# Both feed-forward down projections as seven 2x2 block products over pairs of hidden tiles, with norms by quarters of the tokens

## The chip, the cores and the metric

The kernel runs on one core of a Trainium2 chip, in one launch. The metric is the device time of one execution in microseconds, the median of several runs. TensorE (PE) multiplies, VectorE (DVE), ScalarE (ACT) and GpSimd (POOL) do elementwise work, SyncE (SP) issues nearly all DMAs.

## The reference

One decoder layer over 1024 prompt tokens and 8 single-token samples (1032 columns in all), model width 1024, in float32: a half feed-forward, a token mixer (RWKV-7 and RG-LRU), cross-attention, a second half feed-forward, each followed by a layer norm. The change concerns the two feed-forwards and the norms behind them:

```python
D_MODEL = 1024; D_FF = 2816; DN_ALPHA = 2.0 ** 0.25
def _swiglu(h, wi, wo):
    u = h @ wi
    gate, up = u[..., :D_FF], u[..., D_FF:]
    return (jax.nn.silu(gate) * up) @ wo
h = _layer_norm(DN_ALPHA * h + 0.5 * _swiglu(h, ffn1_wi, ffn1_wo), ln_g[0], ln_b[0])
...
h = _layer_norm(DN_ALPHA * h + 0.5 * _swiglu(h, ffn2_wi, ffn2_wo), ln_g[3], ln_b[3])
```

## The kernel before

Activations lie transposed, features on the 128 partitions and tokens along the free axis: `S.acc` (float32) and its split `S.HH`, `S.HL` are each 8 tiles of 128 x 1032. Every operand of a product is split into a high and a low part in the fp32r type: ACT copies the high part, DVE subtracts it from the raw value (`split`, L225 to L229; `split_half`, L90 to L100), and `mm3` (L122 to L127) issues three matmuls per product, high x high, high x low, low x high. A raw tile comes by DMA into one of a few `raw` buffers.

`ffn` works in two stages. The up projection takes hidden tiles in pairs (`pair`): the 2x2 blocks of weights and activations are combined so that seven block products (the "forms" B11, B21, T1, B22, T2, T3, T4) do the work of eight. POOL forms the weight sums of a pair (`pool_tt`, L334), a product has 258 columns (`HN`, a quarter of the tokens), DVE adds the forms up and multiplies gate by up, and SP writes each finished hidden tile to `HID` in DRAM (L407). A first pair (`classic`) is done without forms, woven with the preceding norm.

The down projection goes tile by tile. The 22 hidden tiles are cut into 8 groups of 2 or 3 (`groups`). `loads` fetches and splits the next group's hidden rows (into HH and HL, for the last group into tiles of its own, `hh` and `hl`) and its weights, while the products of the present one run. For each of 8 output tiles and 3 token thirds of 344 columns (`CH3`) a group is summed in PSUM; the first group is copied, scaled, into `acc` by ACT (L440), the others are added by DVE (L442). Between groups 2 and 5, POOL adds the residual `src`, reloaded by SP, to `acc` (L464). Last, `down_last` takes the last group third by third, and each third's norm is woven with the products of the next one (`weave` steps its streams in proportion).

A norm (`ln_stream`): the sum over feature tiles (L145) goes through a matmul with `ones_d` (L169); DVE subtracts the mean (L181), ACT squares, POOL or DVE adds pairs of squares (L185), PE sums them (L176), a few small steps give the inverse deviation (L192 to L195), PE transposes it (L200), DVE scales (L205), ACT adds the bias (L207); then either the result is written out (second feed-forward) or ACT and POOL split it into HH and HL (L214, L215), which the mixer's products read.

The order within an engine is the order of its queue. It comes from a scheduler that runs over the program in its written order; pools with few buffers (`raw`, `whl`, `xw`, PSUM banks) decide how far loads run ahead. There is no planner of due times.

Of the kernel before, what the change touches and what calls it, by code (L numbers as in the profile page):

```python
# [10 lines left out]
F32 = mybir.dt.float32  # L11
# [8 lines left out]
NT = NP + NS  # L20
# [115 lines left out]
def ln_stat_step(S, st, m, c0, n):  # L136
# [4 lines left out]
    if m == 1:  # L141
        st.s = S.lnp.tile([128, n], F32, tag="lns", name="lns")
# [17 lines left out]
def ln_stream(S, st, li, c0, n, final, keep):  # L160
# [11 lines left out]
    adds = nc.gpsimd if final is None or c0 + n < NT else nc.vector  # L172
# [6 lines left out]
    for k in range(KT):  # L179
        d = acc[:, k, c0:c0 + n]  # L180
        nc.vector.tensor_tensor(out=d, in0=d, in1=mu[:, :n], op=ALU.subtract)  # L181
        sq.append(S.lnp.tile([128, 344], F32, tag="lnq", name="lnq", bufs=3))
# [100 lines left out]
def ffn(S, octx, wi, wo, li, src, pre=(), final=None, keep=None, after=None):  # L283
# [5 lines left out]

    nc, tc = S.nc, S.tc  # L290
    HID = S.dram.tile([JT, 128, NT], F32, name="HID%d" % li)
    with ExitStack() as ctx:
# [39 lines left out]
        gt = pool(uctx, "fg", 6)  # L332
        TT = lambda o, a, b, op: nc.vector.tensor_tensor(out=o, in0=a, in1=b, op=op)
# [30 lines left out]
        def pair(j):  # L364
# [46 lines left out]
        groups = [[0, 1]] + [[3 * g + i for i in (2, 3, 4)] for g in range(5)] + [[17, 18], [19, 20, 21]]  # L411
        hd, wt = {}, {}
        S.hlseq = itertools.cycle([S.whl] * 2 + [S.hlx] * 2)

        def loads(js, to=None):
            for j in js:
                hd[j] = to() if to else (S.HH[:, j % KT, :], S.HL[:, j % KT, :])
                for p in range(2):
                    N = slice(2 * HN * p, 2 * HN * p + 2 * HN)
                    x = raw_tile(S)  # L420
                    nc.sync.dma_start(out=x, in_=HID[j, :, N])
                    split(nc, [t[:, N] for t in hd[j]], x)
                wt[j] = load_split(S, wo[128 * j:128 * j + 128, :])

        loads(groups[0])
        uctx.close()
        S.norms = Norms(S, octx)
        hlast = pool(ctx, "fhl", 3)
        xw = pool(ctx, "fwo", 5)
        S.hlseq = itertools.cycle([S.hlx] * 2 + [xw] * 2 + [S.whl] * 3 + [xw] * 3 + [S.hlx] * 2)  # L430

        def down_tile(js, m, ni, st=None):
            c0, n = CH3[ni]
            q = psum(n)
            for j in js:
                hh, hl = hd[j]
                mm3(nc, q, wblock(wt[j], m), hh[:, c0:c0 + n], hl[:, c0:c0 + n], j == js[0], j == js[-1])
# [5 lines left out]
            if st is not None:  # L443
                ln_stat_step(S, st, m, c0, n)
# [1286 lines left out]
```

## Time and profile before

| | us |
|---|---|
| median of 3 runs (lowest, highest) | 3210.02 (3202.42, 3212.22) |
| the profiled execution, own time | 3199.62 |
| its span | 3197.8 |
| PE busy | 3017.8 (94%) |
| DVE busy | 2197.6 (69%) |
| ACT busy | 1432.7 (45%) |
| POOL busy | 560.2 (18%) |

The profiled execution lies 10.4 us under the median of the runs. A row of the timeline gives an instruction's start and duration in us, counted from the start of the span; a name such as `ps<-HH,wh` is the output and the inputs by the program's names. PE overlaps successive matmuls, so their pitch is read from starts, or from the count in a stretch in which PE is busy all the time. The granted clock (PEclk) is a share of the full 2.4 GHz.

### The profile page before, as it was taken

How to read it: one execution, taken by the hardware profiler on the slowest of the kernel's cores; microseconds unless marked ns; L12 is line 12 of the kernel's file. 1: busy time of each engine (PE TensorE's matmuls, PEld its weight loads, DVE VectorE, ACT ScalarE, POOL GpSimd, SP SyncE). 2: the span in 40 equal slices, each digit the busy share in tenths (PEclk: the TensorE clock that was granted, in tenths of full speed). 3: DMA queues.
4: the chain of work that ended last, by engine and by line, in shares of the span. 5: the costliest groups of instructions: out<-in, count | busy, mean ns of one | idle time of the engine just before them, and what ended most of it. 6: DMA issues, size and time to landing. Idle time of an engine off the chain costs nothing. (4 is left out here: it accounts for less than half of the span.)

```text
span 3197.8 us, 63225 instructions
## 1 busy us (share of the span) xinstructions
PE 3017.8 (94%) x23324; PEld 2848.3 (89%) x23324; DVE 2197.6 (69%) x5895; ACT 1432.7 (45%) x3195; POOL 560.2 (18%) x526
## 2 busy tenths in 40 slices
PE   8999999999999999999999979889997999999997
PEld 8999999999888898888878768778887999999997
DVE  7666665574366888877777877666767666666556
ACT  5333342125465565566555645364235433334212
POOL 2222200132010111010001000250005322220111
PEclk9999999999999999999998969799999999999998
DMA  4222243314644554545454445554433222225321
GB/s 138 80 80 77 80 162 107 110 50 136 207 128 131 152 143 137 143 129 150 138 143 126 131 139 149 178 175 136 150 120 116 71 80 80 80 80 159 107 86 54
DMA packets 391301, 386.72 MB, mean 121 GB/s; under 512 B 153904, under 2 KB 292176, under 8 KB 390992
## 3 DMA queue, kind: packets, MB, share of 16 engines
q1 hardware_dynamic: 390992, 382.69, 39.7%
q8 instruction: 183, 3.00, 0.4%
q14 instruction: 126, 1.03, 0.1%
HBM read 277.54 MB, written 105.23 MB: 120 GB/s over the span
## 5 line engine op out<-in xcount | busy, mean ns | idle before, releaser
L125 PE MATMUL ps<-HH,wh 128*128 128x258 f32 (+1 forms) x2384 | 718.8, 302 | 16.9 <-ACT HH L510 7.4
L126 PE MATMUL ps<-HL,wh 128*128 128x258 f32 (+1 forms) x2384 | 716.9, 301 | 0.1
L127 PE MATMUL ps<-HH,wl 128*128 128x258 f32 (+1 forms) x2384 | 715.8, 300 | 0.0
L125 PE MATMUL g<-HH,wh 128*128 128x344 f32 (+2 forms) x1840 | 624.3, 340 | 14.2 <-DVE acc L442 3.4
L127 PE MATMUL g<-HH,wl 128*128 128x344 f32 (+2 forms) x1840 | 596.2, 325 | 0.5 <-DVE wl L100 0.5
L126 PE MATMUL g<-HL,wh 128*128 128x344 f32 (+2 forms) x1840 | 594.5, 324 | 0.6 <-POOL HL L215 0.5
L125 PEld LDWEIGHTS ps<-HH,wh 128*128 128x128 f32 x2384 | 451.6, 190 | 19.2 <-ACT HH L510 7.4
L126 PEld LDWEIGHTS ps<-HL,wh 128*128 128x128 f32 x2384 | 451.2, 189 | 0.6 <-DVE HL L511 0.5
L127 PEld LDWEIGHTS ps<-HH,wl 128*128 128x128 f32 x2384 | 450.4, 189 | 0.0
L125 PEld LDWEIGHTS g<-HH,wh 128*128 128x128 f32 x1840 | 357.5, 194 | 33.5 <-ACT wh L99 4.6
L126 PEld LDWEIGHTS g<-HL,wh 128*128 128x128 f32 x1840 | 357.8, 195 | 5.3 <-POOL HL L215 1.4
L127 PEld LDWEIGHTS g<-HH,wl 128*128 128x128 f32 x1840 | 355.7, 194 | 4.6 <-DVE wl L100 0.9
L228 ACT ACTIVATE wh<-raw 128x512 fp32r<-128x512 f32 x280 | 176.5, 631 | 321.7 <-PE ps L126 262.5
L334 POOL TENSOR_TENSOR raw<-raw 128x512 f32<-128x512 f32 x160 | 214.1, 1338 | 566.4 <-DVE wl L229 360.1
L229 DVE TENSOR_TENSOR wl<-raw,wh 128x512 fp32r<-128x512 f32 x280 | 201.7, 721 | 137.9 <-ACT wh L228 131.0
L100 DVE TENSOR_TENSOR wl<-raw,wh 128x512 fp32r<-128x512 f32 x302 | 218.7, 731 | 99.9 <-ACT wh L99 97.8
L99 ACT ACTIVATE wh<-raw 128x512 fp32r<-128x512 f32 x302 | 184.6, 625 | 220.1 <-PE ps L126 110.5
L442 DVE SCALAR_TENSOR_TENSOR acc<-ps,acc 128x344 f32<-128x344 f32 x336 | 168.6, 512 | 142.3 <-PE ps L127 141.3
L550 DVE TENSOR_TENSOR pr<-tq,iv 128x2 f32<-128x2 f32 (+30 forms) x496 | 159.8, 322 | 3.2
L555 ACT ACTIVATE ev<-g 128x344 f32<-128x344 f32 x192 | 86.9, 453 | 135.8 <-PE g L127 126.9
L948 DVE TENSOR_REDUCE tq<-pr 128x1 f32<-128x2 f32 (+30 forms) x496 | 120.9, 244 | 2.9
L555 ACT ACT_TABLE_LOAD x93 | 119.3, 1283 | 6.9 <-DVE cs L550 2.9
(410 smaller groups left out, 6303.2 us busy)
## 6 DMA issues: line engine op xcount, KB each, us to landing
raw<-in_wi_dram SPq DMA_DIRECT2D x176, 256.0 KB, 2.6
raw<-in_w_in_dram SPq DMA_DIRECT2D x116, 256.0 KB, 3.3
GD<-ev SPq DMA_DIRECT2D x168, 172.0 KB, 2.5
raw<-in_wo_dram SPq DMA_DIRECT2D x104, 256.0 KB, 3.6
raw<-HID SPq DMA_DIRECT2D x88, 258.0 KB, 3.9
HID<-g SPq DMA_DIRECT2D x80, 258.0 KB, 2.1
tg<-GD SPq DMA_DIRECT2D x32, 512.0 KB, 3.8
wt<-T SPq DMA_DIRECT2D x160, 64.0 KB, 2.8
```

The lines of the kernel that those rows point to most:

```text
L99: nc.scalar.activation(out=hi, in_=raw, func=AF.Identity)
L100: S.low.tensor_tensor(out=lo, in0=raw, in1=hi.bitcast(F32), op=ALU.subtract)
L125: nc.tensor.matmul(ps, wh, xh, start=first, stop=False)
L126: nc.tensor.matmul(ps, wh, xl, start=False, stop=False)
L127: nc.tensor.matmul(ps, wl, xh, start=False, stop=last)
L228: nc.scalar.activation(out=hi, in_=x, func=AF.Identity)
L229: nc.vector.tensor_tensor(out=lo, in0=x, in1=hi.bitcast(F32), op=ALU.subtract)
L334: pool_tt = lambda o, a, b, op: nc.gpsimd.tensor_tensor(out=o, in0=a, in1=b, op=op)
L442: nc.vector.scalar_tensor_tensor(out=a, in0=q, scalar=0.5 / ALPHA, in1=a, op0=ALU.mult, op1=ALU.add)
L550: TTo = lambda o, a, b, op: nc.vector.tensor_tensor(out=o, in0=a, in1=b, op=op)
L555: ACT = lambda o, a, f=AF.Identity, **kw: nc.scalar.activation(out=o, in_=a, func=f, **kw)
L948: nc.vector.tensor_reduce(out=tq[:, 0:m, i], in_=pv, axis=mybir.AxisListType.X, op=ALU.add)
```

## The change

The down projection takes the hidden tiles as 11 pairs and the same seven forms. Of a pair the 2x2 hidden blocks (tile of the pair x left or right quarter of a token half) and the 2x2 weight blocks (tile of the pair x left or right half of the output) are combined. The hidden combinations are formed where the hidden tiles are made (`hidden`, POOL), and all seven go to DRAM as `HF`. Form by form, over two sets of pairs (6, then 5), `prepare` loads and splits the hidden blocks and the weights; the weight sums of T1 are formed by POOL in a buffer `room.w` ("fw") that T2 to T4 read, that of B22 by POOL from a fresh load. A form's products of a set are summed in PSUM, per output tile m (4), token half p (2), and `add` brings the result to `acc`, which now starts as a copy of the residual `src` loaded by 8 DMAs. `room.u` holds the partial sum that several output blocks share. The last two forms of the second set go quarter by quarter with the norms (`finish`), now four norms of 258 columns; `ahead`, which loads the next stage's first weight, comes before the last of them.

```diff
-            for m in range(2):
-                for p in range(2):
-                    nc.sync.dma_start(out=HID[j + m, :, 2 * HN * p:2 * HN * p + 2 * HN], in_=G[m][p])
+            hidden(j // 2, G)
+        def hidden(i, G):
+            T = [ft.tile([128, 2 * HN], F32, tag="t%d" % t, name="t%d" % t) for t in range(4)]
+            sub = lambda o, a, b: pool_tt(o, a, b, ALU.subtract)
+            for p in range(2):
+                (b11, b12), (b21, b22) = ((g[p][:, :HN], g[p][:, HN:]) for g in G)
...
+                for f, b in ((0, b11), (1, b21), (3, b22)):
+                    nc.sync.dma_start(out=HF[i, f, :, N], in_=b)
+                sub(t1, b12, b11)
+                sub(t3, b22, b12)
+                sub(t2, b22, t1)
+                sub(t4, t2, b21)
+            for f, t in zip((2, 4, 5, 6), T):
+                nc.sync.dma_start(out=HF[i, f], in_=t)
...
+        FORMS = ("B11", "B21", "T1", "B22", "T2", "T3", "T4")
+        groups = [range(6), range(6, JT // 2)]
...
+        def prepare(g, f):
+            for n, i in enumerate(groups[g]):
+                x = raw_tile(S)
+                nc.sync.dma_start(out=x, in_=HF[i, f])
...
+                split(nc, hid, x)
+                x = lambda: raw_tile(S)[:, :512]
+                if f < 2:
+                    w = fetch(x(), i, 11 + 10 * f)
+                elif form == "T1":
+                    a11, a21, a22 = (fetch(room.w[:, 3 * n + t], i, b) for t, b in enumerate((11, 12, 22)))
+                    w = x()
+                    pool_tt(w, a21, a22, ALU.add)
+                    pool_tt(a21, a11, a21, ALU.subtract)
+                    pool_tt(a11, a22, a21, ALU.subtract)
+                elif form == "B22":
+                    w = fetch(x(), i, 21)
+                    pool_tt(w, w, room.w[:, 3 * n], ALU.subtract)
+                else:
+                    w = room.w[:, 3 * n + FORMS.index(form) - 4]
+                res.append((wparts(w), hid))
...
+        def add(f, q, m, p, last):
...
+            scaled = lambda o: nc.scalar.activation(out=o, in_=q, func=AF.Identity, scale=sc)
+            onto = lambda o, s=sc: nc.vector.scalar_tensor_tensor(out=o, in0=q, scalar=s, in1=o, op0=ALU.mult,
+                                                                 op1=ALU.add)
+            also = lambda o, x, by=pool_tt: by(o, o, x, ALU.add)
+            if form == "B11":
+                scaled(u)
+                also(c11, u)
+            elif form == "B21":
+                onto(c11)
+            elif form == "T1":
+                v = room.v.tile([128, HN], F32, tag="v", name="v")
+                scaled(v)
+                also(c12, v)
+                also(c22, v)
+            elif form == "B22":
+                onto(c12)
+            elif form == "T2":
+                onto(u)
+                also(c12, u)
+            elif form == "T3":
+                onto(u)
+                also(c22, u, TT if last else pool_tt)
+                also(c21, u)
+            else:
+                onto(c21, -sc)
...
+        for k in range(KT):
+            nc.sync.dma_start(out=S.acc[:, k, :], in_=src[k])
...
+            for p, m in itertools.product(range(2), range(4)):
+                add(f, product(ops, m, p), m, p, False)
...
-        for ni in range(3):
+        for p, f in itertools.product(range(2), (5, 6)):
+            if p and f == 6 and after is not None:
+                ahead(S, after)
             st = SimpleNamespace()
-            weave((down_last(groups[-1], ni, st), KT), *pre)
-            pre = [(ln_finish(S, st, li, *CH3[ni], final, keep), LN_STEPS)]
+            weave((finish(f, p, st), 4), *pre)
+            pre = [(ln_finish(S, st, li, 2 * HN * p + HN * (6 - f), HN, final, keep), LN_STEPS)]
```

POOL's queue before, from the end of the first up projection through its down projection to the first norm of the thirds (`raw` at L334: weight sums of the up projection; L464: the residual; L145 and L185: the norm):

```order
L334 TENSOR_TENSOR raw<-raw 128x512 x77
L464 TENSOR_TENSOR acc<-acc,raw 128x516 x16
L622 MEMSET TT_8799 128x512
L622 MEMSET TT_8800 128x512
L145 TENSOR_TENSOR lns<-lns,acc 128x344
```

Here the only work in the down projection is the sixteen additions of the residual. POOL's queue in the changed kernel, from the last hidden combination (`t3`) to the first weights of T1 (`pool_tt` stands at L337 there; `fu` is `room.u`, `fw` is `room.w`, and the `raw` tile written from `fw` is T1's own weight):

```order
L337 TENSOR_TENSOR t3_6215<-t1_6213,g_5685 128x258
L337 TENSOR_TENSOR acc_6304<-acc_6304,fu_6318 128x258 x8
L337 TENSOR_TENSOR raw_6568<-fw_6314 128x512
L337 TENSOR_TENSOR fw_6314<-fw_6314 128x512 x2
L337 TENSOR_TENSOR raw_6583<-fw_6314 128x512
L337 TENSOR_TENSOR fw_6314<-fw_6314 128x512 x2
L337 TENSOR_TENSOR raw_6598<-fw_6314 128x512
```

The eight additions of B11's result stand ahead of T1's weights, and each of T1's six weight sums is followed by the two sums for T2 and T3. The same queue a little later, from T1's last weight on (`v` is T1's result, added to two output blocks; the `raw` tiles written from `raw` and `fw` are B22's weights):

```order
L337 TENSOR_TENSOR raw_6643<-fw_6314 128x512
L337 TENSOR_TENSOR fw_6314<-fw_6314 128x512 x2
L337 TENSOR_TENSOR acc_6304<-acc_6304,v_6896 128x258 x2
L337 TENSOR_TENSOR acc_6304<-acc_6304,v_6919 128x258 x2
L337 TENSOR_TENSOR raw_6815<-raw_6815,fw_6314 128x512
L337 TENSOR_TENSOR acc_6304<-acc_6304,v_6942 128x258 x2
L337 TENSOR_TENSOR acc_6304<-acc_6304,v_6965 128x258 x2
L337 TENSOR_TENSOR raw_6826<-raw_6826,fw_6314 128x512
L337 TENSOR_TENSOR raw_6837<-raw_6837,fw_6314 128x512
L337 TENSOR_TENSOR acc_6304<-acc_6304,v_6988 128x258 x2
```

B22's weights stand between the additions of T1's results. SP's queue before, at the change from the first up projection to its down projection (L407 writes a hidden tile, L421 loads one back, L94 loads half a weight tile):

```order
L407 DMA HID0_131<-g_5488 128x516
L421 DMA raw_6338<-HID0_131 128x516
L407 DMA HID0_131<-g_5489 128x516
L94 DMA raw_6342<-in_wo1_dram 128x512
L94 DMA raw_6348<-in_wo1_dram 128x512
L421 DMA raw_6354<-HID0_131 128x516
```

SP's queue in the changed kernel at the same place (L419 and L425 write hidden forms, L461 loads one, L447 loads a weight block, L538 the residual):

```order
L419 DMA HF0_132<-g_5685 128x258
L425 DMA HF0_132<-t3_6215 128x516
L461 DMA raw_6373<-HF0_132 128x516
L447 DMA raw_6377<-in_wo1_dram 128x512
L461 DMA raw_6383<-HF0_132 128x516
L538 DMA acc_6304<-in_xT_dram 128x1032 x8
L447 DMA raw_6387<-in_wo1_dram 128x512
L461 DMA raw_6561<-HF0_132 128x516
L447 DMA fw_6314<-in_wo1_dram 128x512 x3
L461 DMA raw_6576<-HF0_132 128x516
L447 DMA fw_6314<-in_wo1_dram 128x512 x6
```

The eight loads of `acc` stand behind the last write of a hidden form and ahead of the first load of `fw`.

## Rows read from the trace of the kernel before

**Rows 1.** The page's head and its busy times by engine (us, share, instructions).
```profile
span 3197.8 us, 63225 instructions
...
PE 3017.8 (94%) x23324; PEld 2848.3 (89%) x23324; DVE 2197.6 (69%) x5895; ACT 1432.7 (45%) x3195; POOL 560.2 (18%) x526
```

**Rows 2.** Windows: busy us and count by engine, clock, DMA share, GB/s.
```profile
core 0: us, PE busy (x) PEld busy (x) DVE busy (x) ACT busy (x) POOL busy (x), PEclk, DMA share, GB/s
160.00:240.00 80.00, 80.00 (x669) 80.00 (x668) 52.78 (x100) 29.05 (x59) 20.99 (x16) 1.00 0.25 80
480.00:640.00 160.00, 160.00 (x1016) 160.00 (x1016) 90.51 (x163) 34.11 (x61) 16.43 (x12) 1.00 0.35 108
```

**Rows 3.** Timeline of PE: start, us, instruction, count, idle before and its releaser.
```profile
460.07 0.32 PE L125 MATMUL ps<-HH,wh 128*128 128x344 f32 x1
...
467.92 0.42 PE L125 MATMUL ps<-HH,wh 128*128 128x344 f32 x1 [2.02 <-ACT acc L440]
...
678.10 0.32 PE L125 MATMUL ps<-hh,wh 128*128 128x344 f32 x1
...
723.76 0.40 PE L127 MATMUL ps<-hh,wl 128*128 128x344 f32 x1
727.59 0.66 PE L125 MATMUL g<-HH,wh 128*128 128x344 f32 x1 [3.43 <-DVE acc L442]
...
3128.29 0.32 PE L125 MATMUL ps<-hh,wh 128*128 128x344 f32 x1
```

**Rows 4.** Timeline of POOL in the first and the second up projection.
```profile
424.27 1.28 POOL L334 TENSOR_TENSOR raw<-raw 128x512 f32<-128x512 f32 x1 [5.64 <-DVE wl L229]
...
2480.66 0.74 POOL L246 TENSOR_TENSOR acc<-acc 128x258 f32<-128x258 f32 x1
```

**Rows 5.** The page's costliest groups: count, busy us, mean ns, idle before.
```profile
L228 ACT ACTIVATE wh<-raw 128x512 fp32r<-128x512 f32 x280 | 176.5, 631 | 321.7 <-PE ps L126 262.5
L334 POOL TENSOR_TENSOR raw<-raw 128x512 f32<-128x512 f32 x160 | 214.1, 1338 | 566.4 <-DVE wl L229 360.1
L229 DVE TENSOR_TENSOR wl<-raw,wh 128x512 fp32r<-128x512 f32 x280 | 201.7, 721 | 137.9 <-ACT wh L228 131.0
```

**Rows 6.** Timeline of DVE at the end of the first up projection.
```profile
462.83 0.42 DVE L333 TENSOR_TENSOR g<-g,c 128x258 f32<-128x258 f32 x1
```

**Rows 7.** The page's DMA issues: count, KB each, median us to landing.
```profile
HID<-g SPq DMA_DIRECT2D x80, 258.0 KB, 2.1
```

**Rows 8.** Windows of 10 us with the most DMA traffic; columns as before.
```profile
10.00:20.00 10.00, 8.74 (x47) 7.90 (x47) 7.26 (x16) 8.31 (x17) 0.00 (x0) 1.00 1.04 342
460.00:470.00 10.00, 7.98 (x51) 7.70 (x51) 7.05 (x15) 6.17 (x14) 0.00 (x0) 1.00 0.88 289
```

**Rows 9.** Timeline of POOL and DVE where the residual is added.
```profile
572.04 1.68 POOL L464 TENSOR_TENSOR acc<-acc,raw 128x516 f32<-128x516 f32 x1 [1.05 <-DVE acc L442]
572.49 1.78 DVE L100 TENSOR_TENSOR wl<-raw,wh 128x512 fp32r<-128x512 f32 x1
```

**Rows 10.** Windows behind the end of the first down projection; columns as before.
```profile
725.00:730.00 5.00, 2.41 (x7) 2.22 (x8) 3.95 (x11) 5.00 (x13) 3.75 (x4) 0.63 0.72 251
730.00:735.00 5.00, 5.00 (x23) 4.71 (x22) 4.13 (x6) 5.00 (x12) 4.47 (x6) 0.69 0.47 147
```

**Rows 11.** Timeline of DVE and ACT in the last norm of the kernel.
```profile
3178.83 1.78 DVE L181 TENSOR_TENSOR acc<-acc,ln 128x344 f32<-128x344 f32 x4 [0.40 <-PE ln L169]
...
3184.92 0.52 DVE L185 TENSOR_TENSOR lnq<-lnq 128x344 f32<-128x344 f32 x1 [0.76 <-ACT lnq L183]
...
3189.71 2.02 DVE L205 SCALAR_TENSOR_TENSOR acc<-acc,lng,ln 128x344 f32<-128x344 f32 x4 [2.48 <-PE ln L200]
...
3194.32 0.58 ACT L207 ACTIVATE acc<-acc,lnb 128x344 f32<-128x344 f32 x1 [0.21 <-DVE acc L205]
```

**Rows 12.** Lines of DVE by form: count, busy us, mean ns, idle before.
```profile
L205 DVE SCALAR_TENSOR_TENSOR acc<-acc,lng,ln 128x344 f32<-128x344 f32 x48 | 24.9, 566 | 10.5 <-PE ln L200 10.5
L205 DVE SCALAR_TENSOR_TENSOR acc<-acc,lng,ln 128x256 f32<-128x256 f32 x48 | 20.7, 470 | 4.0 <-PE ln L200 4.0
```

**Rows 13.** Timeline of PE and POOL in the first feed-forward's last norm.
```profile
710.34 0.82 PE L169 MATMUL ln<-lns,ones_d 128*128 128x344 f32 x2
...
726.25 7.87 POOL L215 TENSOR_TENSOR HL<-acc,HH 128x344 fp32r<-128x344 f32 x8 [3.40 <-ACT HH L214]
```

More of the change, by code (lines that the diff above doesn't have):

```diff
@@ L171, in ln_stream @@
     sq = []
-    adds = nc.gpsimd if final is None or c0 + n < NT else nc.vector
+    adds = nc.gpsimd if final is None or c0 != 2 * HN else nc.vector
     def squares(k):
@@ L290, in ffn @@
     nc, tc = S.nc, S.tc
-    HID = S.dram.tile([JT, 128, NT], F32, name="HID%d" % li)
+    HID = S.dram.tile([2, 128, NT], F32, name="HID%d" % li)
+    HF = S.dram.tile([JT // 2, 7, 128, 2 * HN], F32, name="HF%d" % li)
     with ExitStack() as ctx:
@@ L332, in ffn @@
         gt = pool(uctx, "fg", 6)
+        ft = pool(uctx, "ff", 2)
         TT = lambda o, a, b, op: nc.vector.tensor_tensor(out=o, in0=a, in1=b, op=op)
@@ L409, in ffn @@
         for j in range(2, JT, 2):
             pair(j)
[L411 to L423, printed above, removed]
@@ L425, in ffn @@
-        loads(groups[0])
+            if j == 2:
+                G = [[gt.tile([128, 2 * HN], F32, tag="g%d" % m, name="g", bufs=3) for _ in range(2)] for m in range(2)]
+                for m, p in itertools.product(range(2), range(2)):
+                    nc.sync.dma_start(out=G[m][p], in_=HID[m, :, 2 * HN * p:2 * HN * p + 2 * HN])
+                hidden(0, G)
+        FORMS = ("B11", "B21", "T1", "B22", "T2", "T3", "T4")
+        groups = [range(6), range(6, JT // 2)]
+        slots = [[(6 * f + n) % 16 for n in range(6)] for f in range(7)] + [
+            [10, 11, 12, 13, 14], [15, 0, 1, 2, 3], [4, 5, 6, 7, 8], [9, 0, 1, 2, 3], [10, 11, 12, 13, 14]]
@@ L426, in ffn @@
+        ops = prepare(0, 0)
         uctx.close()
         S.norms = Norms(S, octx)
[L428 to L437, printed above, removed]
-            a = S.acc[:, m, c0:c0 + n]
-            if js[0] == 0:
-                nc.scalar.activation(out=a, in_=q, func=AF.Identity, scale=0.5 / ALPHA)
-            else:
-                nc.vector.scalar_tensor_tensor(out=a, in0=q, scalar=0.5 / ALPHA, in1=a, op0=ALU.mult, op1=ALU.add)
-            if st is not None:
-                ln_stat_step(S, st, m, c0, n)
@@ L465, in ffn @@
-        if after is not None:
-            ahead(S, after)
+        room.w = pool(ctx, "fw", 1).tile([128, 18, 512], F32, name="fw")
+        room.u = pool(ctx, "fu", 1).tile([128, 4, 2 * HN], F32, name="fu")
+        room.v = pool(ctx, "fv", 3)
+        xw = pool(ctx, "fwo", 3)
+        S.hlseq = itertools.cycle([xw] * 3 + [S.hlx] * 4 + [S.whl] * 3)
+        banks = itertools.cycle([ps])
+        for k in range(KT):
+            nc.sync.dma_start(out=S.acc[:, k, :], in_=src[k])
+        order = list(itertools.product(range(2), range(7)))
@@ new lines, in ffn, with finish @@
+        for (g, f), then in zip(order, order[1:]):
+            if then == (1, 5):
+                S.hlseq = itertools.cycle([S.whl] * 3 + [xw] * 2 + [S.hlx] * 4 + [xw])
+            new = prepare(*then)
+            if then == (1, 6):
+                break
+            for p, m in itertools.product(range(2), range(4)):
+                add(f, product(ops, m, p), m, p, False)
+            ops = new
+        ops = [ops, new]
+        def finish(f, p, st):
+            c0 = 2 * HN * p + HN * (6 - f)
+            for m in range(4):
+                ln_stat_step(S, st, m, c0, HN)
+            for m in range(4):
+                add(f, product(ops[f - 5], m, p), m, p, True)
+                ln_stat_step(S, st, 4 + m, c0, HN)
+                yield
```

55 lines of the change are left out of this document (36 added, 19 removed).

## The prediction

> **What bounds the kernel now.** The page comes first: TensorE (PE) is busy 94% of the span, VectorE (DVE) 69%, ScalarE (ACT) 45%, GpSimd (POOL) 18% [rows 1]. A busy PE may still wait, so the second view is the count of matmuls per 80 us [rows 2]. In the up projection 669 block products of 258 columns start in 80 us, one per 119.6 ns; in the down projection 1016 of 344 columns in 160 us, one per 157.5 ns. The clock is 1.00 and PE has no idle time in these stretches: PE alone sets their length. The third view is the timeline at the edges of the down projection [rows 3]. It starts at 460.07 us; PE stands still once for 2.0 us (a wait for the first eviction, which ends at 467.92); its last group of tiles, woven with the norms, begins at 678.10 and ends at 723.76, and the next stage at 727.59 after 3.4 us of waiting. In the second feed-forward the last group begins at 3128.29, and the kernel ends 69.5 us later, because the norms, which are DVE, ACT and POOL work, finish after PE. So a column saved before that last group is worth its full time as long as the other engines deliver in time; inside it, less.
>
> **What it saves on PE.** Before, each down projection is 22 input tiles x 8 output tiles x 3 token thirds x 3 products = 1584, at 157.5 ns 249.5 us. After, it is 7 forms x 11 pairs x 4 x 2 x 3 = 1848 of 258 columns, at 119.6 ns 221.0 us [rows 2]: 28.5 us less. Of this, 1368 against 1608 products lie ahead of the last group (215.5 - 192.3 = 23.2 us) and 216 against 240 in it (34.0 - 28.7 = 5.3 us).
>
> **What it adds in the up projection.** Eight POOL subtractions per pair, 0.74 us each alone [rows 4], 5.9 us in the 40.2 us that a pair's 336 products take; POOL is busy 21.0 of 80 us there [rows 2]. I cost them at nothing: POOL's own weight work takes part of the rest, and the sums are read only in the next stage. The HID writes become ten smaller HF writes per pair on SP, with the DMA engines at 25% [rows 2]. If the cover were gone, a pair could lose at most the 5.9 us.
>
> **What it adds in the down projection.** Per form 6 hidden tiles and 6 weight tiles are split for only 17.2 us of products (144 x 119.6 ns) in the first half, 14.4 us in the second. A split costs ACT 0.63 and DVE 0.72 us [rows 5], so 12 splits and 8 evictions fill under 13 us of a form on either engine: hidden. POOL is the question. T1 needs three 512-wide operations per pair (1.28 us each [rows 4]), B22 one, and T1's results are added twice into acc.
>
> Take the first half, with t = 0 at the last product of the up projection. By the order, SP loads acc only behind the last HF writes, and T1's weights (fw) only behind acc. Before, the last of the hidden values is written by DVE 3.2 us after the change of stages [rows 3, 6]; a POOL subtraction follows (0.74), and a write lands 2.1 us after issue [rows 7], so acc starts at about +6.8. Ahead of POOL's first T1 operation go acc (8 x 0.528 MB), a weight tile, a hidden tile and three fw tiles: 5.54 MB. The busiest stretches move 289 and 342 GB/s [rows 8]; at their middle, 315, this takes 17.6 us: +24.4. By then POOL's eight B11 additions (done at the pace of PE, about +20) are over. The last weight of T1 is POOL's 16th operation: 20.5 us.
>
> Here DVE joins in. A POOL operation of 516 columns took 1.68 us when DVE's splits ran beside it, and a DVE split queued behind it took 1.78 [rows 9]; alone they take 1.28 and about 0.7 [rows 4, 5]. So they can take turns, and a split that meets POOL then costs POOL about 0.38 us. But over the up projection, where DVE splits as well, the 160 POOL operations of this width take 1.338 us on average [rows 5]: 0.06 lost in each. The new stretch is denser in splits than the up projection; I take 0.2 us per split, between the two. In the order 11 splits stand in that stretch: 2.2 us. The weight is ready at +47.1; split and three products (0.63 + 0.72 + 0.36) later T1's first group of products ends, +48.8. Unhindered it would end at two forms and 2.15 us, +36.6. PE waits 12.2 us.
>
> B22 comes from the same queue. Behind T1's last weight stand two more 512-wide operations, twelve additions into acc and the six of B22: 2.6 + 8.9 + 7.7 = 19.2 us, with 12 splits between them 2.4 more, then 1.7: B22's first group ends at +70.4 instead of +53.8. The lag is 16.6 us in all. Behind it no form waits for POOL's 512-wide work until the second half. That one's fifteen operations (19.2 us) have B11 and B21 of the second half as cover, 28.7 us, besides T4: nothing; were the cover gone, each late microsecond would be one of PE.
>
> Off this go the 2.0 us that PE stands at the same place before [rows 3]: 14.6. A pause costs more than itself: after the 3.8 us without matmuls at 723.76 the granted clock is 0.63 and 0.69 in the next two stretches of 5 us [rows 10], so some 3.4 us went at 1.2 instead of 2.4 GHz in each; one such spell of 3.4 us delays products by 1.7. T1's spell is hidden, since B22 waits for POOL anyway, so I add 1.7 once: 16.3 us.
>
> Bounds of this lag: with no turns lost and acc and weights in time, POOL starts at +20, and B22's first group ends at 20 + 20.5 + 19.2 + 1.7 = +61.4: 7.6 - 2.0 = 5.6 us. With 289 GB/s (+26.0) and a whole 0.72 lost per split, it ends at 26.0 + 20.5 + 7.9 + 19.2 + 8.6 + 1.7 = +83.9: 30.1 - 2.0 + 1.7 = 29.8. I take 16.3, since rows 9 show a price and the mean in rows 5 a small one.
>
> The Trainium skill ("SBUF — State Buffer", section "Who interferes with whom") says that a DVE instruction with two SBUF inputs and a GpSimd instruction that reads SBUF exclude each other for the whole instruction. Rows 9 agree that they wait for each other, but show about 0.4 us lost to POOL, not a whole split, and the mean in rows 5 still less. By the rule in full the lag would be near its upper bound, and the change a loss; that is the second rival below.
>
> **The tails.** Four norms of 258 columns replace three of 344. Each has a part that does not shrink: from the end of the last sum of squares (3184.92 + 0.52) to the first scaled value at 3189.71, 4.3 us [rows 11]. In the second feed-forward the last norm's elementwise work (3178.83 to 3185.4 and 3189.71 to 3194.9, 11.8 us) shrinks by 470/566, as the 256- and 344-wide rows of L205 stand [rows 12]: 2.0. So -5.3 + 4.3 - 2.0 = -3.0 us. In the first, a norm took 23.8 us from its mean product (710.34) to its last low part (726.25 + 7.87) [rows 13]; a quarter would take 19.8. The mixer's first third has its quarters in time, but its second third needs the last one, whose cover is now one third's tiles, 4 x 24 x 157.5 ns = 15.1 us and some 4 us of the norm's own products, instead of two: 1 us short. -5.3 + 4.3 + 1.0 = 0. Either tail could be 5 us off both ways.
>
> **The sum,** against the profiled execution's own 3199.6 us: 2 x (-23.2 + 16.3) = -13.8, tails -3.0 and 0: -16.8, so 3182.8. The median of the runs shown lies 10.4 us above that execution: 3193.
>
> **Rivals.**
> A. *The preparation stays hidden.* For it: ACT and DVE have room, SP may issue fw as soon as acc has left, and the mean of 1.338 us shows that it mostly works unhindered. Against it: its 512-wide operations and additions stand in one queue. At the lower bound, 2 x (-23.2 + 5.6) - 3.0 = -38.2: 3161.4, on the scale of the runs 3172.
> B. *POOL's queue becomes the bound of the first half.* With 0.72 us lost per split and 289 GB/s the lag is 29.8: 2 x 6.6 - 3.0 = +10.2, 3220 on the scale of the runs; later HF writes, or POOL work that spills into the second half, would come on top. It is slower from a lag of 29.5 us per feed-forward on. For it: rows 9 show the turns, and the order gives POOL no other place. Against: POOL lost less than that in rows 9, and far less on average.
> C. *Four norms cost more than three.* Two fixed chains of 4.3 us more in each tail, because the quarters' chains don't overlap the products as the thirds' did: 17.2 us, 3210. The fixed chain speaks for it, the narrower work against it.
>
> **How the numbers follow.** 0.3% (9.6 us) is about what a measurement of this kernel can tell from no change. The forecast has 0.45, with its own range 3181 to 3206: 0.29 of it is faster than 3200.4, 0.16 within. A has 0.22 (faster), B 0.22 (slower), C 0.11 (within). So faster 0.51, same 0.27, slower 0.22. The range 3165 to 3226 leaves out the outer parts of A and of B.
>
> **What would show it.** 1848 products at 119.6 ns per projection, away from T1 and B22. In each first half two pauses of PE: T1's first group waits for wl, released by POOL, for 9 to 15 us, and B22's for 3 to 7; POOL busy without a break for some 50 us there, its 512-wide operations at 1.4 to 1.6 us, and the clock near 0.65 behind the pause. No pause in the second half. A lag under 10 us or above 23 would make the forecast wrong, and so would the clock staying low for longer than one such spell or a loss in the up projection.

## The result and the profile after

The changed kernel took 3237.64 us (median; 3230.09 to 3241.34), the kernel before 3209.63 us beside it: a ratio of 1.0092 (95% interval 1.0075 to 1.0108), some 29.5 us slower, where 17 us less were forecast and a range of 3165 to 3226 given. The profiled executions, whose rows follow, stand 35.4 us apart in their spans (3197.8 and 3233.2 us).

The head of the page and three of its costliest groups, beside [rows 1, 5], and two groups of the lines by form (count | busy us, mean ns | idle before):

```profile
span 3233.2 us, 65577 instructions
...
PE 2997.9 (93%) x23910; PEld 2822.3 (87%) x23910; DVE 2321.4 (72%) x5915; ACT 1505.4 (47%) x3383; POOL 971.1 (30%) x954
...
L229 DVE TENSOR_TENSOR wl<-raw,wh 128x512 fp32r<-128x512 f32 x368 | 336.4, 924 | 191.9 <-ACT wh L228 186.3
...
L337 POOL TENSOR_TENSOR raw<-raw 128x512 f32<-128x512 f32 x160 | 216.1, 1351 | 304.0 <-DVE wl L229 168.9
...
L229 DVE TENSOR_TENSOR HL<-raw,HH 128x516 fp32r<-128x516 f32 x154 | 149.4, 996 | 26.7 <-ACT HH L228 26.4
```

```profile
L337 POOL TENSOR_TENSOR fw<-fw 128x512 f32<-128x512 f32 x44 | 68.7, 1567 | 2.7
L337 POOL TENSOR_TENSOR acc<-acc,v 128x258 f32<-128x258 f32 x64 | 59.4, 957 | 4.1 <-ACT v L502 4.1
```

PE is 19.9 us less busy although products of 28.5 us per projection are gone (a slow clock counts as busy). POOL has 411 us more. DVE's splits of weights have gone from 721 to 924 ns, but these are means over the whole kernel, and 280 of the 368 splits lie in the up projections. By stretch (lines by form): the first down projection in the changed kernel (460 to 640 us), then before (460 to 680), and last the first up projection (80 to 460), changed and before:

```profile
L229 DVE TENSOR_TENSOR HL<-raw,HH 128x516 fp32r<-128x516 f32 x51 | 52.3, 1048 | 10.0 <-ACT HH L228 10.0
L229 DVE TENSOR_TENSOR wl<-raw,wh 128x512 fp32r<-128x512 f32 x35 | 39.2, 1146 | 31.2 <-ACT wh L228 30.9
...
L100 DVE TENSOR_TENSOR wl<-raw,wh 128x512 fp32r<-128x512 f32 x41 | 30.4, 751 | 13.6 <-ACT wh L99 13.0
L229 DVE TENSOR_TENSOR HL<-raw,HH 128x516 fp32r<-128x516 f32 x30 | 22.3, 753 | 12.9 <-ACT HH L228 12.8
...
L229 DVE TENSOR_TENSOR wl<-raw,wh 128x512 fp32r<-128x512 f32 x131 | 114.1, 877 | 59.9 <-ACT wh L228 58.1
...
L229 DVE TENSOR_TENSOR wl<-raw,wh 128x512 fp32r<-128x512 f32 x126 | 89.6, 711 | 65.3 <-ACT wh L228 62.0
```

A split of a loaded tile takes 1.05 to 1.15 us in the down projection instead of 0.75, and 0.88 instead of 0.71 in the up projection. The windows (columns as in [rows 2]):

```profile
160.00:240.00 80.00, 80.00 (x669) 80.00 (x668) 57.95 (x100) 28.95 (x60) 35.44 (x32) 1.00 0.31 100
500.00:510.00 10.00, 6.40 (x28) 5.69 (x28) 6.95 (x8) 2.31 (x4) 9.69 (x7) 0.66 0.06 15
520.00:530.00 10.00, 6.07 (x40) 4.98 (x38) 5.60 (x6) 3.93 (x9) 10.00 (x11) 0.83 0.51 155
530.00:540.00 10.00, 6.65 (x26) 5.72 (x26) 10.00 (x11) 8.03 (x17) 7.29 (x6) 0.50 0.67 172
550.00:570.00 20.00, 20.00 (x170) 20.00 (x169) 12.15 (x22) 7.83 (x15) 5.60 (x7) 1.00 0.52 175
670.00:690.00 20.00, 11.80 (x95) 11.58 (x95) 18.85 (x60) 7.38 (x14) 7.57 (x9) 0.84 0.14 34
```

The up projection keeps its 669 products per 80 us, as in [rows 2], and 550 to 570 shows the pace of the new products. Between them PE stands, and behind its pauses the granted clock is 0.66, 0.83 and 0.50 (0.50 is the lower level, 1.2 GHz, all the time), while POOL is busy 73 to 100%. The third place, 670 to 690, is in the second half, where no pause was forecast, and there POOL is not the busy one: DVE is. PE's rows there (timeline, as in [rows 3]):

```profile
459.56 0.28 PE L127 MATMUL ps<-T4h,wl 128*128 128x258 f32 x1
...
529.24 0.58 PE L125 MATMUL ps<-HH,wh 128*128 128x258 f32 x1 [2.45 <-ACT wh L228]
...
534.74 0.58 PE L127 MATMUL ps<-HH,wl 128*128 128x258 f32 x1 [1.82 <-DVE wl L229]
...
632.02 0.39 PE L125 MATMUL ps<-HH,wh 128*128 128x258 f32 x1 [1.93 <-DVE acc L503]
...
689.12 0.58 PE L127 MATMUL ps<-HH,wl 128*128 128x258 f32 x1 [8.20 <-DVE wl L229]
...
746.60 0.63 PE L125 MATMUL g<-HH,wh 128*128 128x344 f32 x1
...
3159.61 0.58 PE L127 MATMUL ps<-HH,wl 128*128 128x258 f32 x1 [3.50 <-DVE wl L229]
```

From the last up product to the mixer's first it took 287.0 us (746.60 - 459.56), before 267.6 (727.59 - 459.95, where the row at 460.07 in [rows 3] follows at once). Of the 35.4 us between the spans, 19.4 arise there, 5.6 until the second feed-forward's last up product (the end of the norms slows the mixer's start), 10.8 behind it.

For the experiments a mark is useful: the start of DVE's first addition in the norm-woven part, `acc<-acc,fu`, which follows T3's first product group of the second half, counted from 0.12 us behind the start of the last up product. With products alone it would stand at about 194.5 us (1608 + 15 products at 119.6 ns, and DVE's addition from PSUM into `fu` behind them). In the changed kernel it stands at 234.0 and 228.8 us (first and second feed-forward).

### The profile page after: what moved, and what is told of

The parts are those of the page before. It is cut to its first block, busy times and chain, and to the rows that moved or that the text cites. A ratio compares the mean times of both kernels' runs of the same rounds, so it can differ in the third digit from the quotient of the medians.

```text
span 3233.2 us, 65577 instructions
## 1 busy us (share of the span) xinstructions
PE 2997.9 (93%) x23910; PEld 2822.3 (87%) x23910; DVE 2321.4 (72%) x5915; ACT 1505.4 (47%) x3383; POOL 971.1 (30%) x954
## 5 line engine op out<-in xcount | busy, mean ns | idle before, releaser
L125 PE MATMUL ps<-HH,wh 128*128 128x258 f32 (+1 forms) x2704 | 783.7, 291 | 31.8 <-ACT wh L228 14.0
L127 PE MATMUL ps<-HH,wl 128*128 128x258 f32 (+1 forms) x2704 | 780.0, 289 | 22.7 <-DVE wl L229 22.7
L126 PE MATMUL ps<-HL,wh 128*128 128x258 f32 (+1 forms) x2704 | 780.3, 289 | 6.7 <-DVE HL L229 6.0
L125 PEld LDWEIGHTS ps<-HH,wh 128*128 128x128 f32 x2704 | 520.5, 193 | 36.7 <-ACT wh L228 16.3
L127 PEld LDWEIGHTS ps<-HH,wl 128*128 128x128 f32 x2704 | 518.6, 192 | 26.8 <-DVE wl L229 26.7
L126 PEld LDWEIGHTS ps<-HL,wh 128*128 128x128 f32 x2704 | 520.2, 192 | 8.4 <-DVE HL L229 6.9
L229 DVE TENSOR_TENSOR wl<-raw,wh 128x512 fp32r<-128x512 f32 x368 | 336.4, 924 | 191.9 <-ACT wh L228 186.3
L337 POOL TENSOR_TENSOR raw<-raw 128x512 f32<-128x512 f32 x160 | 216.1, 1351 | 304.0 <-DVE wl L229 168.9
L100 DVE TENSOR_TENSOR wl<-raw,wh 128x512 fp32r<-128x512 f32 x214 | 155.1, 730 | 83.3 <-ACT wh L99 82.3
L229 DVE TENSOR_TENSOR HL<-raw,HH 128x516 fp32r<-128x516 f32 x154 | 149.4, 996 | 26.7 <-ACT HH L228 26.4
L893 POOL TENSOR_TENSOR ivc<-ivc,mhalf 128x4 f32<-128x4 f32 x32 | 32.7, 1023 | 392.7 <-DVE ivc L649 335.6
L893 POOL TENSOR_TENSOR ivs<-ivs,mhalf 128x4 f32<-128x4 f32 x32 | 33.2, 1039 | 379.5 <-DVE ivs L649 180.7
```

What stands on the lines that cost most here:

```text
L100: S.low.tensor_tensor(out=lo, in0=raw, in1=hi.bitcast(F32), op=ALU.subtract)
L125: nc.tensor.matmul(ps, wh, xh, start=first, stop=False)
L126: nc.tensor.matmul(ps, wh, xl, start=False, stop=False)
L127: nc.tensor.matmul(ps, wl, xh, start=False, stop=last)
L229: nc.vector.tensor_tensor(out=lo, in0=x, in1=hi.bitcast(F32), op=ALU.subtract)
L337: pool_tt = lambda o, a, b, op: nc.gpsimd.tensor_tensor(out=o, in0=a, in1=b, op=op)
```

## The experiments

| kernel | ratio to before (interval) | marks, us |
|---|---|---|
| changed | 1.0092 (1.0075 to 1.0108) | 234.0, 228.8 |
| e1 other ring of buffers | 1.0111 (1.0096 to 1.0126) | 234.6, 229.7 |
| e2 quarters in the kernel before | 1.0037 (1.0025 to 1.0048) | |
| e3 no weight sums | 0.9928 (0.9910 to 0.9945) | 208.0, 202.4 |
| e4 no load of acc | 1.0088 (1.0073 to 1.0103) | 229.9, 226.1 |
| e5 additions on DVE | 1.0006 (0.9993 to 1.0018) | 220.4, 214.5 |
| e8 early chain | 1.0070 (1.0049 to 1.0090) | 229.3, 229.0 |
| e9 e5, T1's sum on DVE, e1, e8 | 0.9990 (0.9979 to 1.0001) | 214.0, 213.1 |
| e10 e9 without e1 | 0.9990 (0.9980 to 1.0000) | 213.2, 214.2 |
| e11 T4 third | 1.0057 (1.0035 to 1.0079) | 226.9, 221.1 |
| e12 e10 with e11 | 0.9999 (0.9988 to 1.0011) | 217.5, 215.4 |
| e13 e10, acc later | 1.0000 (0.9987 to 1.0012) | 217.2, 214.3 |

**e3, POOL's weight sums left out.**

```diff
-                    w = x()
-                    pool_tt(w, a21, a22, ALU.add)
-                    pool_tt(a21, a11, a21, ALU.subtract)
-                    pool_tt(a11, a22, a21, ALU.subtract)
+                    w = a21
...
-                    pool_tt(w, w, room.w[:, 3 * n], ALU.subtract)
```

> Edit: the changed kernel without POOL's weight sums of T1 and B22 (left out of the computation: the forms take the loaded weight blocks as they are; all loads, splits and products stay). In the changed kernel 220.6 us pass from the last up product to the end of T2 of the second half, in either feed-forward, where 1608 products at 119.6 ns fill 192.3. Theory, POOL's queue makes the lag of 28 us: without the sums the stretch takes 195 to 202 us, and the kernel 40 to 50 us less than the changed one, near 3190. Rival, the DMA queue makes it (acc, fw and hidden loads at 380 to 400 GB/s): the stretch stays at 212 us or more, and less than 20 us are won.

The marks fall by 26.0 and 26.4 us, the time by 1.64% of 3210 us, 52.6 us, somewhat more than the theory's 40 to 50: 26.3 per projection are POOL's sums. DVE's rows of the marks in the changed kernel, and in this one:

```profile
693.64 0.43 DVE L336 TENSOR_TENSOR acc<-acc,fu 128x258 f32<-128x258 f32 x1
...
3164.19 0.43 DVE L336 TENSOR_TENSOR acc<-acc,fu 128x258 f32<-128x258 f32 x1
```

```profile
668.87 0.43 DVE L336 TENSOR_TENSOR acc<-acc,fu 128x258 f32<-128x258 f32 x1
...
3104.05 0.43 DVE L336 TENSOR_TENSOR acc<-acc,fu 128x258 f32<-128x258 f32 x1
```

The theory's own stretch, to the end of T2, took 198.7 us, inside its 195 to 202, and the rival (transfers) falls: all loads are still there. But 6.4 of these us, and 13.5 and 7.9 at the marks, are behind the products without any sum: not everything is POOL's.

**e4, acc filled with zeros by POOL instead of loaded.**

```diff
-            nc.sync.dma_start(out=S.acc[:, k, :], in_=src[k])
+            nc.gpsimd.memset(S.acc[:, k, :], 0.0)
```

> Edit: the changed kernel without the load of the residual into acc (left out of the computation: POOL fills acc with zeros instead; 4.2 MB less traffic at the start of each down projection). POOL's first weight sum of T1 starts 26.5 us after the last up product in the changed kernel. Theory, POOL's queue is the bound from there on: it can start some 8 to 11 us earlier, so that 5 to 10 us per feed-forward are won, 3218 to 3228. Rival, transfers are not what POOL waits for (it also waits for B11's results): the first sum starts less than 4 us earlier, and under 5 us are won in all. Rival, transfers alone make the lag: more than 15 us per feed-forward are won.

POOL's first sum started 6 us earlier (+20.8 instead of +26.9), the marks fell by 4.1 and 2.7 us, and the time can't be told from the changed kernel's. The theory asked for more (8 to 11 us earlier, 5 to 10 us won per feed-forward). The prediction had made the load of acc and fw the start of the chain. What the load costs by itself this run doesn't show: the zeros take 8 instructions of POOL's own queue (7.28 us), and PE's pause at B21's last weights is 5.83 and 6.39 us long where the changed kernel has 1.42 and 1.99; just before it ACT's queue waits 8.75 us for one of POOL's sums.

**e5, the additions of B11 and T1 by DVE from PSUM.**

```diff
                 scaled(u)
-                also(c11, u)
+                onto(c11)
...
-                v = room.v.tile([128, HN], F32, tag="v", name="v")
-                scaled(v)
-                also(c12, v)
-                also(c22, v)
+                onto(c12)
+                onto(c22)
```

> Edit: the changed kernel, but B11's and T1's results go into acc by DVE straight from PSUM (scalar_tensor_tensor, 0.41 us) instead of by POOL from a copied tile: 24 POOL additions of 258 columns fewer per half, 24 DVE instructions more; the weight sums stay on POOL. In the changed kernel T3's first result of the second half is added 234.0 us after the last up product in the first feed-forward and 228.8 in the second (208.0 and 202.4 without any weight sums). Theory, POOL's queue is one line in which additions and sums add up: B22's weights, which stood behind 16 additions of some 0.9 us, come 12 to 15 us earlier, the mark falls to 216 to 222 and 212 to 217, and the kernel takes some 25 us less than the changed one, about as long as the kernel before. Rival, DVE is the one that is full: it gets 10 us more per half, its splits get later, the marks stay within 5 us and the time too.

As the theory said, marks and time: 0.86% less than the changed kernel, some 28 us. The rival falls: DVE has 24 additions more per half, and still its splits of `fw` take 736 ns on average instead of 823, and PE's wait of 3.50 us in the second feed-forward is gone (in the first 4.41 us of 8.20 are left). With the sums untouched, taking other work out of the same queue gives as much as half of the sums. The rows of POOL's queue in the changed kernel show why, from T1's last sums to B22's last (start, us, count):

```profile
486.56 1.29 POOL L337 TENSOR_TENSOR raw<-fw 128x512 f32<-128x512 f32 x1 [5.92 <-DVE acc L503]
...
509.27 1.74 POOL L337 TENSOR_TENSOR raw<-fw 128x512 f32<-128x512 f32 x1
511.08 3.33 POOL L337 TENSOR_TENSOR fw<-fw 128x512 f32<-128x512 f32 x2
514.37 3.36 POOL L337 TENSOR_TENSOR acc<-acc,v 128x258 f32<-128x258 f32 x4
517.69 1.28 POOL L337 TENSOR_TENSOR raw<-raw,fw 128x512 f32<-128x512 f32 x1
518.94 3.34 POOL L337 TENSOR_TENSOR acc<-acc,v 128x258 f32<-128x258 f32 x4
...
529.68 3.39 POOL L337 TENSOR_TENSOR raw<-raw,fw 128x512 f32<-128x512 f32 x2
533.04 4.25 POOL L337 TENSOR_TENSOR acc<-acc,v 128x258 f32<-128x258 f32 x4
```

POOL works without a break from 486.56 on, and PE's last pause at B22 ends at 534.74, one split behind the sum that ends at 533.07.

**e1, another ring of split-weight buffers.**

```diff
-        S.hlseq = itertools.cycle([xw] * 3 + [S.hlx] * 4 + [S.whl] * 3)
+        S.hlseq = itertools.cycle([xw] + [S.whl] * 3 + [S.hlx] * 2 + [xw] * 2 + [S.hlx] * 2)
...
-            if then == (1, 5):
-                S.hlseq = itertools.cycle([S.whl] * 3 + [xw] * 2 + [S.hlx] * 4 + [xw])
```

> Edit: the changed kernel, but the ring of split-weight buffers is ordered so that T3's weights of the second half get buffers that B22 has left, not those that T2 still reads. In the profile of the changed kernel PE waits 8.20 us (first feed-forward) and 3.50 us (second) at the first product of that T3 for a low weight part. Theory: this wait is made by the ring (a T3 split can only start when the last T2 product is done) and lengthened by what stands ahead of it in DVE's queue; with the ring changed both waits fall under 1 us and, with the low clock behind them, about 10 us go in the first and 5 us in the second feed-forward: some 15 us less than the changed kernel, near 3222. Rival, the quarter norms are what costs in the tails: the waits only move to the norms, and the time stays within 5 us of 3237.

Both waits for T3's weights went, and nothing was won. PE's rows in this kernel, at the first norm's mean:

```profile
700.67 1.20 PE L169 MATMUL ln<-lns,ones_d 128*128 128x258 f32 x2 [6.71 <-DVE lns L145]
...
3167.36 0.67 PE L169 MATMUL ln<-lns,ones_d 128*128 128x258 f32 x2 [3.26 <-POOL acc L337]
```

The theory (the ring) falls: nothing of its 15 us came. The waits moved to the norm, as the rival said, but that the quarters cause them doesn't follow, since the norms are the same in both kernels; e2 has their price. The wait belongs to DVE and POOL, which are late there; here the next product that needed them waited.

**e8, the mixer's chain of small instructions at the start of the kernel.**

```diff
+    lam = S.const.tile([128, 8], F32, name="lam")
+    nc.sync.dma_start(out=lam, in_=I["vec"][:, 10, :])
+    ...
+    S.sp = sp8, nsp8
...
-        sp8, nsp8 = cp.tile([128, 8], F32, name="sp8"), cp.tile([128, 8], F32, name="nsp8")
...
-        TSC(nsp8, sa, -4.0, None, ALU.mult, None)
+        sp8, nsp8 = S.sp
```

> Edit: the changed kernel, but a chain of some 30 DVE instructions of 8 columns (a softplus of the mixer's constants) is computed at the start of the kernel instead of standing in DVE's queue behind the first feed-forward, where it lies among T2's results and ahead of T3's weights. Theory: this chain is why PE waits 8.20 us for T3's weight in the first feed-forward and 3.50 in the second, where there is no such chain; without it the first wait falls to 3 to 4 us, and 5 to 7 us go. Rival, DVE is late there anyway and the wait only moves behind the norm's mean, as when the buffers were changed: under 2 us go.

The first feed-forward's wait fell from 8.20 to 2.88 us and its mark by 4.7, the second's stayed at 3.50 and 229.0. The ratio fell by 0.22%, 7 us, which its interval alone would not tell from nothing; the profile does. In the changed kernel DVE's queue had held T3's splits behind that chain (timeline):

```profile
686.84 0.16 DVE L649 TENSOR_SCALAR nsp<-spt 128x8 f32<-128x8 f32 x1
686.91 0.42 DVE L503 SCALAR_TENSOR_TENSOR fu<-ps,fu 128x258 f32<-128x258 f32 x1
687.25 3.02 DVE L229 TENSOR_TENSOR wl<-fw,wh 128x512 fp32r<-128x512 f32 x4
```

**e2, the norms and the last group by quarters, in the kernel before.**

```diff
-            c0, n = CH3[ni]
+            c0, n = (HN * ni, HN) if st is not None else CH3[ni]
...
-        for ni in range(3):
+        for ni in range(4):
...
-            pre = [(ln_finish(S, st, li, *CH3[ni], final, keep), LN_STEPS)]
+            pre = [(ln_finish(S, st, li, HN * ni, HN, final, keep), LN_STEPS)]
```

> Edit: the kernel before, with only its last group of products and the norms cut into four quarters of 258 columns (one part of the change alone). The tail from the last group's first product to the end is 69.5 us before and, from T3's first product on, 77.2 us in the changed kernel (second feed-forward); to the mixer's first product 49.5 and 65.9 us (first). Theory: the quarters themselves cost little, since the work per column is the same and each norm adds one fixed chain of 4.3 us, partly hidden: 0 to 5 us more per tail, 3210 to 3220 in all, most of it in the second feed-forward. Rival, the quarter norms make the tails long: 8 us and more per tail, 3226 or more.

11.9 us (8 to 15): the quarters cost something by themselves, a little more than the 10 us that the theory allowed and less than the rival's 16. Against the theory, more of it lies behind the first feed-forward: in the profiles 7.0 us there (5.1 before the mixer's first product, 1.9 after it) and 3.9 in the second.

**e9 and e10, POOL relieved further.** Both have e5's edit, e8's, and

```diff
-                    pool_tt(w, a21, a22, ALU.add)
+                    TT(w, a21, a22, ALU.add)
```

and e9 has e1's ring as well.

> Edit: the changed kernel with the additions of B11 and T1 on DVE, T1's own weight sum on DVE too (POOL keeps two sums per pair for T2 and T3 and one for B22), the other ring of split-weight buffers, and the early chain. Theory, POOL's queue made the lag: POOL's work ahead of B22's weights falls from 18 sums, 24 additions and 6 sums to 12 and 6 sums (some 25 us, due by 51.6 us after the last up product), the marks fall to 206 to 212 and 200 to 207, and the kernel is faster than the one before: a ratio of 0.990 to 0.996. Rival, DVE becomes the bound (24 additions and 6 sums more per half, 14 us): marks at 220 or more, ratio 1.00 or more.

> Edit: as the one with additions and T1's sum on DVE and the early chain, but with the ring of split-weight buffers as in the changed kernel. Theory: with DVE less held up by POOL, the wait for T3's weight in the second half is 2 us or less even so, and the time is within 3 us of the one with the other ring. Rival, the ring binds by itself: PE waits 3 us or more there, in both feed-forwards, and 6 us or more are lost against the other ring.

These are the fastest complete versions, 1.0% under the changed kernel and about level with the one before. The gain of 0.4 to 1.0% expected of e9 was missed, and its rival's case (marks at 220, ratio 1.00) didn't come either: the marks stay 19 us behind 194.5. That the ring doesn't matter, e10's theory, was right: the times are equal, and PE's pauses there are under 1 us in both.

**e11 and e12, T4 third in the first half,** in the changed kernel and in e10; T4's weight needs no sum, so T1's are due one form later.

```diff
+        seq = [(0, 1, 6, 2, 3, 4, 5), range(7)]
...
-                nc.sync.dma_start(out=x, in_=HF[i, f])
+                nc.sync.dma_start(out=x, in_=HF[i, seq[g][f]])
...
-                    a11, a21, a22 = (fetch(room.w[:, 3 * n + t], i, b) for t, b in enumerate((11, 12, 22)))
+                    a11, a21, a22 = (room.w[:, 3 * n + 2] if t == 2 and not g else fetch(room.w[:, 3 * n + t], i, b)
+                                     for t, b in enumerate((11, 12, 22)))
...
+                elif form == "T4" and not g:
+                    w = fetch(room.w[:, 3 * n + 2], i, 22)
```

> Edit: the changed kernel with one step moved: in the first half the forms go B11, B21, T4, T1, B22, T2, T3, so that T4, whose weight is a loaded block and needs no sum, gives POOL 17.2 us more before T1's weights are due. POOL's work is the same, instruction for instruction; only its due time moves. Theory, the lag is POOL's queue against its due time: T1 is due 51.6 us after the last up product instead of 34.4, POOL's eighteenth sum was done at 54.7 us; of the lag of 24 us in the first half 13 to 17 go, the marks (first result of T3 of the second half) fall from 234.0 and 228.8 us to 217 to 221 and 212 to 216, and the kernel takes 25 to 34 us less than the changed one, a ratio of 0.998 to 1.002 to the one before. Rival, it is what POOL and DVE cost each other whenever both work (splits of 1.78 us), not a due time: the lag only moves to later forms, and under 10 us in all are won.

> Edit: T4 third in the first half, with the additions of B11 and T1 and T1's own sum on DVE, and the early chain (the ring of buffers as in the changed kernel). Of the 19 to 20 us by which the marks lay behind the ideal 194 us with DVE's additions alone, some 14 stood between 39 and 67 us, at T1 and B22. Theory, due time again: they go, marks near 200, and 25 us less than without the step, 0.990 to 0.993 of the kernel before. Rival, DVE's splits for T1 (its sum among them) are the bound by then: marks at 208 or more, and a ratio of 0.996 or more.

e11 won 7.1 and 7.7 us in the marks, half of the theory's, a result between it and the rival's: POOL's first sum also started later, 36 instead of 27 us after the last up product, because two of T1's blocks are now loaded behind T4's tiles. Its row here (the last up product started at 461.10), then ACT's wait and PE's pause in e12:

```profile
497.12 1.41 POOL L337 TENSOR_TENSOR raw<-fw 128x512 f32<-128x512 f32 x1 [13.10 <-DMA fw<-in_wo_dram]
```

```profile
524.91 0.64 ACT L228 ACTIVATE HH<-raw 128x516 fp32r<-128x516 f32 x1 [10.33 <-DMA raw<-HF]
...
528.08 0.58 PE L125 MATMUL ps<-HH,wh 128*128 128x258 f32 x1 [7.16 <-ACT wh L228]
```

In e12, ACT idled 10.33 us for a hidden tile just before the wait: the loads have become late, not POOL. It won nothing against e10, so its theory falls; the marks at 215 to 218 and the ratio are those of its rival, whose reason (DVE's splits) the rows don't bear out.

**e13, acc loaded behind B21's tiles** (in e10, with B11's and B21's results added together).

```diff
-        for k in range(KT):
-            nc.sync.dma_start(out=S.acc[:, k, :], in_=src[k])
...
+            for k in range(KT if then == (0, 1) else 0):
+                nc.sync.dma_start(out=S.acc[:, k, :], in_=src[k])
```

> Edit: as the kernel with DVE's additions, T1's sum on DVE and the early chain (forms in the changed kernel's order, ratio 0.999), and in addition acc is loaded behind B21's hidden and weight tiles instead of ahead of them, and B11's result is added to acc by DVE together with B21's, so that nothing in the first 17 us waits for acc. Theory: the pauses of 1.4 to 1.9 us at +24 us (B21's weights, loaded behind 4.2 MB of acc) go in both feed-forwards, with the low clock behind them, and T1's, which wait for fw behind acc, stay: 4 to 8 us in all, a ratio of 0.996 to 0.998. Rival, fw comes later by as much as B21's loads move ahead (3.1 MB, 8 us), and T1's pause at +41 us grows by what is won: 0.998 to 1.002.

The rival's case: the pause at +24 us went, the ones from +37 us on grew (1.3, 2.3 and 1.9 us instead of 1.0 and 1.8). So B21's pause came from the load of acc ahead of its weights: B21's form now ends 2.0 and 1.8 us behind the products, in e10 5.8 and 4.0.

## Why the prediction was wrong

In the scale of the time before: products -57.0 us (counted, as predicted), sums on POOL +52.6 (e3), quarters +11.9 (e2), together +7.5; +29.5 was measured, so 22.0 us remain (give or take some 7, by the intervals of e2 and e3). e3's marks, 13.5 and 7.9 us behind the products, show 21.4 us of such delay without any sum, of which the stop in the kernel before (2.0 us in the first) explains little.

Where a projection falls behind can be counted: PE's rows hold all its 1848 products, and without a pause each would start 119.6 ns behind the one before. The first product of T2 in the first half, the 577th, would then stand 68.9 us behind the first one. Its row in the changed kernel (first product at 459.68) and in e3 (460.83):

```profile
553.08 0.28 PE L125 MATMUL ps<-HH,wh 128*128 128x258 f32 x1
```

```profile
535.99 0.28 PE L125 MATMUL ps<-HH,wh 128*128 128x258 f32 x1
```

That is a lag of 24.5 us, and of 6.3 without sums. Counted in the same way (us, first and second feed-forward):

| lag behind the products | changed kernel | e3 | forecast |
|---|---|---|---|
| behind B21, first half | 3.2, 4.1 | 5.7, 5.7 | 0 |
| behind B22, first half | 24.5, 24.6 | 6.3, 6.3 | 18.3 |
| behind T2, second half | 28.3, 27.2 | 6.4, 6.4 | 18.3 |
| at the mark (T3, second half) | 39.5, 34.3 | 13.5, 7.9 | 18.3 |

The marks are 73.8 us late in all, and 36.6 were forecast: 37.2 us too few, 12.5 of them in the first halves and 24.7 in the second.

- *The up projection costs nothing*: right; 669 products in 80 us, the last one at 459.56 us.
- *POOL makes a lag in the first half*: right in mechanism and place, T1 and B22; the size was off, 24.5 us for 18.3 (16.6 and a spell of low clock). The sums' share of it is 18.2 (24.5 less e3's 6.3); that this is the forecast's figure is luck, since the forecast is the whole lag. The terms: POOL's first sum at +26.9 instead of +24.4 (whose own parts, 3.2, 0.74 and 2.1 us, make a start at +6.0 and not +6.8); sixteen of them 24.5 us (486.56 to 511.01) instead of 22.7, since a sum lost 0.29 us (mean 1567 against 1280 ns), not the 0.14 that 0.2 us for each of 11 splits make; from there to B22's last sum 22.1 instead of 21.6. These give 21.4 us, and the other 3.1 are the clock, for which 1.7 had been added: the two stretches in [rows 10] lie one behind the other, so they are one spell of twice the length. The two long pauses forecast came as ten short ones of 0.4 to 2.5 us, together 5.0 us at T1 (for 9 to 15) and 7.0 at B22, with the clock at 0.66, 0.83 and 0.50 in the windows above.
- *The splits are hidden: 12 splits and 8 evictions fill under 13 us of a form on either engine*, and with it *no pause in the second half*. This step failed, and no rival covered it. It took durations from a stage in which POOL works a quarter of the time. The price of the turns that POOL and DVE take falls on DVE as well: 1048 and 1146 ns for a split in the first down projection instead of 753 and 751, DVE busy 18.85 of 20 us at 670. So DVE's queue ran late in the second half: 1.93 us for a PSUM bank, and 8.20 and 3.50 for T3's weights, which with the low clock behind them are 15.0 and 9.7 us of lag. e1 shows that these waits are no matter of one buffer; e5 that they shrink when POOL has less to do and DVE more; e8 that 5 us of the first came from a chain of 8-column instructions, which had been harmless as long as nothing urgent stood behind it in DVE's queue (it ran at 662 to 676 us in the kernel before, and PE had no pause there).
- *B11 and B21 of the first half* were given no lag. They have 3.2 and 4.1 us of it, 5.7 without the sums; e13 puts B21's part down to the load of acc. With T3's 7.1 and 1.5 us this is nearly all of the 21.4 us that e3 leaves.
- *The tails*: the quarters without the saved products were put at 5.3 and 2.3 us (4.3 + 1.0, 4.3 - 2.0), 7.6 in all; e2 gives 11.9. A term mis-sized by 4 us. Rival C, four norms as the reason of a level time, was too strong in its 17.2.
- Rival B was nearest: slower, with POOL as the bound of the first half. But its lag of 29.8 us (with the stop of 2.0 before taken off) was too long: the first half's is 22.5 on that scale, with which its sum stays level. What spilled into the second half it named only as something on top, without a price, so it had the direction right in part by luck. Its price, a whole split lost per meeting, was not the cause of its direction: POOL lost 0.29 us per sum, and DVE the rest.

The Trainium skill ("SBUF — State Buffer", section "Who interferes with whom") says that the order of issue, not the shape of the operation, decides which of the two engines blocks. The rows agree that both pay: POOL's sums rose by 0.29 us on average, DVE's splits in the first down projection by 0.30 and 0.40. The prediction had counted such a loss in POOL's queue alone. No run here took the turns away without taking work away, so what they cost apart from the work is argued and not shown.

What stays open: e9, e10, e12 and e13 all end 19 to 23 us behind the products in the marks, wherever T1 or acc stands. e12's rows name the hidden tiles' loads, e13's the loads of fw and DVE's sums; which of SP's order, the few raw buffers and DVE's splits holds them was not tried. That some of the 22.0 us is the clock after each pause is read from the windows, not tested by itself.

## What to carry over

Work that is moved to an idle engine has to be set against its due time in that engine's queue, with everything else that stands in the queue, and against what it does to the engine with which it takes turns: here 44 sums per projection took back 26.3 of the 28.5 us that the products saved. Take durations from a stretch in which the same neighbours are busy. A wait that is taken away where an engine is late can move to the next instruction that needs it, as in e1; look at how far behind its own inputs the engine is before mending one wait.

## What was not expected of the hardware

The price of a meeting fell on DVE as much as on POOL. DVE's rows in the first half of the changed kernel, while POOL is busy and just after:

```profile
530.20 3.43 DVE L229 TENSOR_TENSOR HL<-raw,HH 128x516 fp32r<-128x516 f32 x2
...
539.58 0.68 DVE L229 TENSOR_TENSOR wl<-fw,wh 128x512 fp32r<-128x512 f32 x1
```

Two splits took 1.7 us each beside POOL's sums, one 0.68 after them. In the up projection, where the two meet as well, POOL's 160 sums kept 1351 ns on average, and there it was DVE alone that paid: 877 ns for a split instead of 711, with room to spare. A mean from one stage did not carry to another with the same widths.
